# Rotary queries kept by feature: the rotation on whole tiles, heads put together by DMA

## The chip, the cores and the metric

The kernel runs on one core of a Trainium2 chip. The metric is the device time of one execution in microseconds, taken as the median of several runs. The core has a matrix engine (TensorE, PE in the profile; its weight loads are listed as PEld), VectorE (DVE), ScalarE (ACT), GpSimd (POOL) and SyncE (SP), each with an instruction queue of its own that is worked off in order. DMAs are issued from the queues of SP, ACT and POOL.

## The reference, cut to what matters

The reference is one layer with two token mixers side by side, gated linear attention (GLA) and multi-head latent attention (MLA), and a feed-forward block behind them. There are 512 tokens of width 1024. The change concerns MLA's rotary part:

```python
def apply_rope(x, cos, sin):
    half = x.shape[-1] // 2
    xf = x.astype(jnp.float32)
    x1, x2 = xf[..., :half], xf[..., half:]
    return jnp.concatenate([x1 * cos - x2 * sin, x2 * cos + x1 * sin], axis=-1).astype(x.dtype)
...
    q = (rms_norm(q_lat, q_a_norm_g) @ w_q_b).reshape(bsz, seq, MLA_HEADS, MLA_QK)
    q_nope = q[..., :MLA_NOPE]
    q_rope = apply_rope(q[..., MLA_NOPE:], cos[:, :, None], sin[:, :, None])
    c_kv = rms_norm(kv_lat[..., :MLA_KV_RANK], kv_a_norm_g)
    k_rope = apply_rope(kv_lat[..., MLA_KV_RANK:], cos, sin)
...
    s = (jnp.einsum('bhqd,bhkd->bhqk', q_nope[:, :, q0:q1], k_nope[:, :, :q1])
         + jnp.einsum('bhqr,bkr->bhqk', q_rope[:, :, q0:q1], k_rope[:, :q1]))
```

There are eight heads. Each head's query has 128 plain features and 64 rotary ones; `q_lat` has rank 384. The rotary key of 64 features is shared by the heads.

## The kernel before, in words

**Numbers.** Almost every product is made in three matmuls on operands that are split into a high part (rounded by ACT) and a low part (the rest, subtracted by DVE): high by high, high by low, low by high. `split` does this for a tile. Weights come by SP's queue into `wraw`, are split into `whi` (line L189) and `wlo` (L190) by `pump`, which runs ahead of the products by one entry of a list (`stream`), and by two entries with the loads. The buffers for these are two or three each, so a split waits for the product that last read its buffer.

**Two forms of product.** `gemm_fm` keeps the weights as the stationary operand and gives features on the partitions, 512 tokens wide (L245 to L247). `gemm_tm` keeps the activations stationary and gives tokens on the partitions (L279 to L281), for the rotary queries 256 columns wide: four heads of 64. Both collect in PSUM: four banks of the pool `mm` for products and four of the pool `px` for transposes, scores and the like.

**The order of the work.** The program names its steps one by one, with generators (`spawn`, `tick`) that are stepped between the products; a scheduler that estimates durations then fixes the order on each engine, and the engines follow that order. The stages that matter here: the latents with `latents2` (normalisation, rotary key) among the query, key and value projections of GLA, some 80 to 125 us into the run; the GLA levels beside them (`gla_levels`, L849, with POOL's sums L787 and L788); then the gates (`unit`, L1172 to L1174), which end near 307 us; then `mla_qr(0)`, the first group of four heads; `y_gla(0)`, a projection into four PSUM banks; the first pair of heads; `mla_qr(1)`; `y_gla(1)`; three more pairs.

**Rotary queries before.** `mla_qr` makes, for each of four tiles of 128 tokens, the four heads' rotary features side by side (two token tiles share one PSUM bank). `ev_qr` rotates them on DVE with the tables `cs2` and `sn2`, which have tokens on the partitions (L521 to L523), adds on POOL (L524), and splits the result into `q2` (L114, L115), high and low part beside each other for every head. `tr` then turns each head by four PE transposes (L946) with the rounded identity `identr` and copies it on ACT into `QS` (L949): 128 partitions, of which the upper half is the low part. The scores use `QS` as the stationary operand against the two layers of `KK` (L987, L988).

**Rotary key before.** After the rotation the key is rounded twice into `krh` (L634) and its rest put into `krl` beside zeros (L635, cleared by POOL at L632). Each is transposed in four steps (L642, L646) and copied into `KK` (L643, L648): layer 0 holds the high part twice, layer 1 the low part over zeros.

Of the kernel before, what the change touches and what calls it, by code (L numbers as in the profile page):

```python
# [10 lines left out]
F32 = mybir.dt.float32  # L11
F32R = mybir.dt.float32r
# [19 lines left out]
NOPE = 128  # L32
ROPE = 64
HQ = NOPE + ROPE
# [18 lines left out]
def tile_hybrid_block(ctx: ExitStack, tc: tile.TileContext, I, out, dbg=None):  # L53
    nc = tc.nc
# [12 lines left out]
        uid[0] += 1  # L67
        return f"{s}_{uid[0]}"

    TAG_C = ('h0', 'qn', 'PT1', 'res', 'bc', 'T1', 'T2')  # L70
# [58 lines left out]
    ident = ca[:, 0:P]  # L129
# [4 lines left out]
    identr = consts.tile([P, P], F32R, name="identr")  # L134
# [6 lines left out]
    DMA_AHEAD, SPLIT_AHEAD = 2, 1  # L141
    later = {}

    def plan(name, c0, n, k_lo=0, k_hi=None, heads=None, res=False, per=2):
        w = I[name]
        K = w.shape[0] // P
        k_hi = K if k_hi is None else k_hi
        idx = []
        for k0 in range(k_lo, k_hi, per):
            nk = min(per, k_hi - k0)  # L150
            if heads is None:
                src = w.rearrange("(k p) n -> p k n", p=P)
                dmas = [(slice(0, nk), src[:, k0:k0 + nk, c0:c0 + n], None)]
            else:
                hw, h0, nh = heads
                src = w.rearrange("(k p) (h c) -> p k h c", p=P, c=hw)
                cw = n // nh
                dmas = [(kk, src[:, k0 + kk, h0:h0 + nh, c0:c0 + cw], cw) for kk in range(nk)]
            idx.append(len(stream))
            stream.append({"dmas": dmas, "nk": nk, "n": n, "res": res})  # L160
        return {"idx": idx, "nk": k_hi - k_lo, "per": per}

    def fetch(n):
        while st["dma"] < min(len(stream), n):
            e = stream[st["dma"]]
            st["dma"] += 1
            if "src" in e:
                continue
            raw = A([P, e["nk"], T * 2 // e["nk"]], F32, "wraw")
            for sl, src, cw in e["dmas"]:  # L170
                dst = raw[:, sl, :e["n"]]
                if cw is not None:
                    dst = dst.rearrange("p (h c) -> p h c", c=cw)
                nc.sync.dma_start(dst, src)
            e["raw"] = raw

# [33 lines left out]
    def spawn(g):  # L210
        active.append(g)
        return g
# [87 lines left out]
    PL = {}  # L300
# [25 lines left out]
    PL["v", 1] = plan("w_in", C_V + T, T)  # L326

    def plan_qr(g):
        PL["qr", g] = plan("w_q_b", NOPE, 4 * ROPE, heads=(HQ, 4 * g, 4))


    HOME = {"w": ("whi", "wlo"), "r": ("wraw", "wraw"), "a": ("xh", "xl")}
# [187 lines left out]
    def rope(src, cs, sn, dst, tmp, tmp2):  # L520
        vtt(tmp, src, cs, op=ALU.mult)  # L521
        vtt(tmp2[..., 0:32], src[..., 32:64], sn[..., 0:32], op=ALU.mult)
        vtt(tmp2[..., 32:64], src[..., 0:32], sn[..., 32:64], op=ALU.mult)  # L523
        gtt(dst, tmp, tmp2, op=ALU.add)  # L524
# [92 lines left out]
    def latents2():  # L617
        yield from rms_T(LQ, QR, qag, qlT, qld)
        qlT.clear()
        kr = B([P, NT, ROPE], F32, "kr")  # L620
        kt1 = B([P, NT, ROPE], F32, "kt1")
        kt2 = B([P, NT, ROPE], F32, "kt2")
        for tt in range(NT):
            src = lat[tt][:, LKR:LKR + ROPE]
            vtt(kt1[:, tt], src, cs2[:, tt], op=ALU.mult)
            vtt(kt2[:, tt, 0:32], src[:, 32:64], sn2[:, tt, 0:32], op=ALU.mult)
            vtt(kt2[:, tt, 32:64], src[:, 0:32], sn2[:, tt, 32:64], op=ALU.mult)
        vtt(kr, kt1, kt2, op=ALU.add)
# [12 lines left out]
        for tt in range(NT):  # L641
            nc.tensor.transpose(p[:, tt * P:(tt + 1) * P], krh[:, tt].rearrange("p a b -> p (a b)"), identr)  # L642
        act(KK[:, 0, :], f(p), AF.Copy)  # L643
        p = PX(dt=F32R)
        for tt in range(NT):
            nc.tensor.transpose(p[:, tt * P:(tt + 1) * P], krl[:, tt].rearrange("p a b -> p (a b)"), identr)  # L646
        yield
        act(KK[:, 1, :], f(p), AF.Copy)  # L648
        KKs.append(KK)


# [269 lines left out]
    QS = [None] * MH  # L921
    scale = HQ ** -0.5

    def mla_qr(g):
        qst = []

        def ev_qr(a, j, ps):
            src = ps[:, :4 * ROPE].rearrange("p (h c) -> p h c", c=ROPE)
            csb = cs2[:, a, None, :].to_broadcast([P, 4, ROPE])
            snb = sn2[:, a, None, :].to_broadcast([P, 4, ROPE])  # L930
            if a == 0:
                pump(PL["qr", g]["idx"][-1] + 1)
            t1 = B([P, 4, ROPE], F32, "rt1")
            t2 = B([P, 4, ROPE], F32, "rt2")
            with tc.issue_after(st["lo"].ins):
                rope(src, csb, snb, t1, t1, t2)
            q2 = B([P, 4, 2, ROPE], F32R, "q2")
            split(t1, q2[:, :, 0, :], q2[:, :, 1, :], scale=scale)
            qst.append(q2)
        gemm_tm([PL["qr", g]], qlT, 4 * ROPE, ev_qr)  # L940

        def tr():
            for h in range(4):
                p = PX(dt=F32R)
                for tt in range(NT):
                    nc.tensor.transpose(p[:, tt * P:(tt + 1) * P], qst[tt][:, h].rearrange("p a b -> p (a b)"), identr)  # L946
# [700 lines left out]
```

## Time and profile before

| what | value |
|---|---|
| runs | 886.94, 887.67, 888.92 us |
| median | 887.67 us |
| span of the profiled execution | 884.5 us |
| PE busy | 868.1 us, 98% |
| DVE busy | 638.4 us, 72% |
| ACT busy | 473.6 us, 54% |
| POOL busy | 185.7 us, 21% |
| instructions | 13143 |

The profile is that of one execution; its span runs from the first to the last instruction on the core. No separate device time of that execution is given, so the span is set beside the median of the runs, 3.2 us above it. Matmuls overlap in the pipeline, so their durations add up to more than their time; what one costs is read from the distance between the starts of neighbours.

### The profile page before, as it was taken

How to read it: one execution, taken by the hardware profiler on the slowest of the kernel's cores; microseconds unless marked ns; L12 is line 12 of the kernel's file. 1: busy time of each engine (PE TensorE's matmuls, PEld its weight loads, DVE VectorE, ACT ScalarE, POOL GpSimd, SP SyncE). 2: the span in 40 equal slices, each digit the busy share in tenths (PEclk: the TensorE clock that was granted, in tenths of full speed). 3: DMA queues.
4: the chain of work that ended last, by engine and by line, in shares of the span. 5: the costliest groups of instructions: out<-in, count | busy, mean ns of one | idle time of the engine just before them, and what ended most of it. 6: DMA issues, size and time to landing. Idle time of an engine off the chain costs nothing.

```text
span 884.5 us, 13143 instructions
## 1 busy us (share of the span) xinstructions
PE 868.1 (98%) x4916; PEld 760.3 (86%) x4916; DVE 638.4 (72%) x1019; ACT 473.6 (54%) x834; POOL 185.7 (21%) x200
## 2 busy tenths in 40 slices
PE   6999999999999999999999999999999999999996
PEld 5988888889999988888888888988888888889985
DVE  7859879959665646646866797887557646788865
ACT  6556676556475534435654414566357546656820
POOL 1314457854201010100000003004400520141000
PEclk9999999999999999999999999999999999999999
DMA  7995936795737423112307528006941990399312
GB/s 247 283 221 152 324 110 162 229 215 168 215 87 194 144 78 102 54 54 63 99 19 268 191 72 285 1 1 167 291 113 29 261 254 28 85 232 231 121 61 81
DMA packets 91023, 132.50 MB, mean 150 GB/s; under 512 B 8992, under 2 KB 54432, under 8 KB 90960
## 3 DMA queue, kind: packets, MB, share of 16 engines
q1 hardware_dynamic: 70672, 92.36, 32.5%
q0 software_dynamic: 18368, 35.66, 18.8%
q10 hardware_dynamic: 1920, 3.66, 1.2%
q8 instruction: 38, 0.62, 0.3%
q14 instruction: 25, 0.20, 0.1%
HBM read 110.15 MB, written 8.91 MB: 135 GB/s over the span
## 4 chain that ended last, share of the span: by engine, by line
PE 98%; DMA 1%; ACT 0%; DVE 0%; POOLq 0%; issue 0%; DVEq 0%; ACTq 0%
PE mm L247 11%; PE mm L245 11%; PE mm L246 11%; PE mm L279 6%; PE mm L280 6%; PE mm L281 6%; PE mm L1172 4%; PE mm L1174 4%; PE mm L1173 4%; PE px L1460 2%; PE px L1458 2%; PE px L1459 2%; PE px L849 2%; PE mm L1460 2%; PE mm L1458 2%; PE mm L1459 2%
## 5 line engine op out<-in xcount | busy, mean ns | idle before, releaser
L190 DVE TENSOR_TENSOR wlo<-wraw,whi 128x1024 fp32r<-128x1024 f32 (+1 forms) x90 | 100.1, 1112 | 91.4 <-ACT whi L189 86.6
L189 ACT ACTIVATE whi<-wraw 128x1024 fp32r<-128x1024 f32 (+1 forms) x90 | 85.5, 950 | 81.3 <-PE mm L246 34.7
L246 PE MATMUL mm<-h,whi 128*128 128x512 f32 x224 | 87.2, 389 | 0.0
L245 PE MATMUL mm<-h,whi 128*128 128x512 f32 x224 | 87.1, 390 | 0.0
L247 PE MATMUL mm<-h,wlo 128*128 128x512 f32 x224 | 83.2, 390 | 0.0
L190 DVE TENSOR_TENSOR wlo<-wq,whi 128x1024 fp32r<-128x1024 f32 x44 | 54.5, 1239 | 30.0 <-ACT whi L189 30.0
L1477 POOL DMA_DIRECT2D res<-ev x42 | 37.4, 1000 | 180.7 <-ACT ev L1475 151.5
L189 ACT ACTIVATE whi<-wq 128x1024 fp32r<-128x1024 f32 x44 | 46.5, 1057 | 27.1 <-PE mm L1173 19.0
L1173 PE MATMUL mm<-sh,whi 128*128 128x256 f32 x176 | 49.9, 283 | 0.0
L1172 PE MATMUL mm<-sh,whi 128*128 128x256 f32 x176 | 49.9, 283 | 0.0
L1174 PE MATMUL mm<-sh,wlo 128*128 128x256 f32 x176 | 49.8, 283 | 0.0
L247 PEld LDWEIGHTS mm<-h,wlo 128*128 128x128 f32 x224 | 42.0, 188 | 9.1 <-DVE wlo L190 0.4
L246 PEld LDWEIGHTS mm<-h,whi 128*128 128x128 f32 x224 | 42.0, 188 | 8.8
L245 PEld LDWEIGHTS mm<-h,whi 128*128 128x128 f32 x224 | 42.0, 188 | 8.6
L189 ACT ACTIVATE xh<-wraw 128x1024 fp32r<-128x1024 f32 (+1 forms) x28 | 27.5, 987 | 28.0 <-PE mm L281 15.8
L429 POOL TENSOR_TENSOR mv<-mv,mhalf 128x1 f32<-128x1 f32 x4 | 3.3, 837 | 170.4 <-DVE mv L428 170.4
L190 DVE TENSOR_TENSOR xl<-wraw,xh 128x1024 fp32r<-128x1024 f32 (+1 forms) x28 | 31.3, 1129 | 8.7 <-ACT xh L189 8.7
L793 ACT ACTIVATE E<-rp 128x256 f32<-128x256 f32 x64 | 25.8, 418 | 20.5 <-POOL rp L788 13.7
L1520 ACT ACTIVATE relu<-mm 128x512 f32<-128x512 f32 x24 | 14.1, 596 | 42.0 <-PE mm L247 42.0
L788 POOL TENSOR_TENSOR rp<-rp 128x256 f32<-128x256 f32 x32 | 33.0, 1030 | 9.8 <-ACT q L818 6.1
L787 POOL TENSOR_TENSOR rp<-rp 128x256 f32<-128x256 f32 x32 | 29.6, 926 | 25.3 <-ACT E L793 18.1
L1174 PEld LDWEIGHTS mm<-sh,wlo 128*128 128x128 f32 x176 | 33.8, 192 | 0.0
(472 smaller groups left out, 2821.4 us busy)
## 6 DMA issues: line engine op xcount, KB each, us to landing
wraw<-in_w_ff_dram SPq DMA_DIRECT2D x36, 512.0 KB, 4.8
wraw<-in_w_in_dram SPq DMA_DIRECT2D x30, 512.0 KB, 4.7
wq<-in_w_ff_dram POOLq DMA_DIRECT2D x26, 512.0 KB, 9.4
res<-ev POOLq DMA_DIRECT2D x42, 256.0 KB, 9.4
wq<-in_w_in_dram SPq DMA_DIRECT2D x20, 512.0 KB, 6.6
wq<-in_w_in_dram POOLq DMA_DIRECT2D x18, 512.0 KB, 9.9
hsd<-hs SPq DMA_DIRECT2D x16, 256.0 KB, 3.8
xr<-hsd SPq DMA_DIRECT2D x16, 256.0 KB, 3.7
```

What stands on the lines that cost most here:

```text
L189: st["ins"] = act(hi[:, :nk, :n], raw[:, :nk, :n], AF.Copy)
L190: st["lo"] = vtt(lo[:, :nk, :n], raw[:, :nk, :n], f(hi[:, :nk, :n]), op=ALU.subtract)
L245: mm(o, hi[:, c], xh, start=first, stop=False)
L246: mm(o, hi[:, c], xl, start=False, stop=False)
L247: mm(o, lo[:, c], xh, start=False, stop=last)
L279: mm(o, xh, hi[:, :n], start=opens, stop=False, skip_group_check=share)
L280: mm(o, xh, lo[:, :n], start=False, stop=False, skip_group_check=share)
L281: mm(o, xl, hi[:, :n], start=False, stop=last, skip_group_check=share)
L1172: mm(oa, hi[:, k, c], xh, start=opens and k == 0 and a == 0, stop=False, skip_group_check=True)
L1173: mm(oa, hi[:, k, c], xl, start=False, stop=False, skip_group_check=True)
L1174: mm(oa, lo[:, k, c], xh, start=False, stop=k == 3, skip_group_check=True)
L1477: nc.gpsimd.dma_start(res[tt + t][:, j * T:(j + 1) * T], e, accum_op=ALU.add)
```

## The change

The products of the rotary queries are turned round: `gemm_fm` with the weights as the stationary operand, so that features stand on the partitions and 512 tokens in the row. So that the rotation needs no partner from another partition, the weights of a group are loaded in two blocks of 128 columns: the first halves of the four heads' features, then the second halves (`parts=2`, 32 columns of each head to a piece, two DMAs where there was one). Each block's product is one PSUM bank.

The rotation is then made on whole tiles of 128x512 with tables that have features on the partitions. `tables` makes them once, ahead of the first group: ACT repeats cosine and sine for four heads, PE transposes them in eight steps with the plain identity, ACT copies them into one tile `tab` of the tag C, which also holds other large tiles. DVE makes two products and a sum for each half (the sum was POOL's), and `split` gives the high and low parts, four tiles `q2`.

The heads are put together by 16 DMAs a group from POOL's queue, each moving 32 partitions of a `q2` tile, 64 KB, into a `QS` tile. The transposes of the queries and their ACT copies are gone.

The rotary key is transposed once, before it is split: four transposes of 64 features, two ACT copies for the two halves of layer 0, one DVE subtraction for the low part. POOL clears the lower half of layer 1.

```diff
     def fetch(n):
...
             for sl, src, cw in e["dmas"]:
-                dst = raw[:, sl, :e["n"]]
-                if cw is not None:
-                    dst = dst.rearrange("p (h c) -> p h c", c=cw)
+                if cw is None:
+                    dst = raw[:, sl, :e["n"]]
+                else:
+                    dst = raw[:, sl[0], sl[1]].rearrange("p (h c) -> p h c", c=cw)
                 nc.sync.dma_start(dst, src)
...
     def plan_qr(g):
-        PL["qr", g] = plan("w_q_b", NOPE, 4 * ROPE, heads=(HQ, 4 * g, 4))
+        PL["qr", g] = plan("w_q_b", NOPE, 4 * ROPE, heads=(HQ, 4 * g, 4), parts=2)
...
-        krh = B([P, NT, 2, ROPE], F32R, "krh")
-        krl = B([P, NT, 2, ROPE], F32R, "krl")
-        nc.gpsimd.memset(f(krl[:, :, 1, :]), 0.0)
-        for i in range(2):
-            act(krh[:, :, i, :], kr, AF.Copy)
-        vtt(krl[:, :, 0, :], kr, f(krh[:, :, 0, :]), op=ALU.subtract)
-        yield
         yield from rms_T(LKV, KVR, kvg, ckT, ckd)
         ckT.clear()
         KK = A([P, 2, T], F32R, "KK")
-        p = PX(dt=F32R)
+        nc.gpsimd.memset(f(KK[ROPE:, 1, :]), 0.0)
+        p = PX()
         for tt in range(NT):
-            nc.tensor.transpose(p[:, tt * P:(tt + 1) * P], krh[:, tt].rearrange("p a b -> p (a b)"), identr)
-        act(KK[:, 0, :], f(p), AF.Copy)
-        p = PX(dt=F32R)
-        for tt in range(NT):
-            nc.tensor.transpose(p[:, tt * P:(tt + 1) * P], krl[:, tt].rearrange("p a b -> p (a b)"), identr)
-        yield
-        act(KK[:, 1, :], f(p), AF.Copy)
+            nc.tensor.transpose(p[:ROPE, tt * P:(tt + 1) * P], kr[:, tt], ident)
+        yield
+        for i in range(2):
+            act(KK[i * ROPE:(i + 1) * ROPE, 0, :], p[:ROPE], AF.Copy)
+        vtt(KK[:ROPE, 1, :], p[:ROPE], f(KK[:ROPE, 0, :]), op=ALU.subtract)
         KKs.append(KK)
...
+    tabs = []
+
+    def tables():
+        tab = A([P, 2, T], F32, "tab")
+        for i, (src, c0) in enumerate(((cs2, 0), (sn2, 32))):
+            p, w = PX(), B([P, NT, 4, 32], F32, "tabw")
+            act(w, src[:, :, None, c0:c0 + 32].to_broadcast([P, NT, 4, 32]), AF.Copy)
+            for tt in range(NT):
+                nc.tensor.transpose(p[:, tt * P:(tt + 1) * P], w[:, tt].rearrange("p a b -> p (a b)"), ident)
+            act(tab[:, i], p, AF.Copy)
+        tabs.append(tab)
+
     def mla_qr(g):
...
-        gemm_tm([PL["qr", g]], qlT, 4 * ROPE, ev_qr)
-
-        def tr():
+        if g == 0:
+            tables()
+        cos, sin = tabs[0][:, 0], tabs[0][:, 1]
+        ps = []
+
+        def ev_qr(a, p):
+            ps.append(p)
             if a == 0:
                 pump(PL["qr", g]["idx"][-1] + 1)
...
+                return
+            parts = []
+            for i, (x, y, op) in enumerate(((ps[0], ps[1], ALU.subtract), (ps[1], ps[0], ALU.add))):
+                t1 = B([P, T], F32, "rt1")
+                t2 = B([P, T], F32, "rt2")
+                with tc.issue_after(st["lo"].ins):
+                    vtt(t1, x, cos, op=ALU.mult)
+                    vtt(t2, y, sin, op=ALU.mult)
+                    vtt(t1, t1, t2, op=op)
+                q2 = [B([P, T], F32R, "q2") for _ in range(2)]
+                split(t1, *q2, scale=scale)
+                parts.append(q2)
             for h in range(4):
-                p = PX(dt=F32R)
-                for tt in range(NT):
-                    nc.tensor.transpose(p[:, tt * P:(tt + 1) * P], qst[tt][:, h].rearrange("p a b -> p (a b)"), identr)
-                yield
                 q = B([P, T], F32R, "QS")
-                act(q, f(p), AF.Copy)
+                for w in range(2):
+                    for i in range(2):
+                        r = (2 * w + i) * 32
+                        nc.gpsimd.dma_start(f(q[r:r + 32]), f(parts[i][w][32 * h:32 * h + 32]))
                 QS[4 * g + h] = q
-        return spawn(tr())
+        gemm_fm(PL["qr", g], qlT, 4 * ROPE, ev_qr)
```

Counted over the whole program: PE loses 72 matmuls of 256 columns and 40 rounded transposes and gains 36 matmuls of 512 columns and 12 plain f32 transposes; POOL loses 8 sums and gains 32 DMA issues; SP issues 12 DMAs for these weights where it issued 6.

More of the change, by code (lines that the diff above doesn't have):

```diff
@@ L68, in nm @@
         return f"{s}_{uid[0]}"
-    TAG_C = ('h0', 'qn', 'PT1', 'res', 'bc', 'T1', 'T2')
+    TAG_C = ('h0', 'qn', 'PT1', 'res', 'bc', 'T1', 'T2', 'tab')
     TAG_W = {'wraw': 3, 'whi': 2, 'wlo': 2}
@@ L142, in tile_hybrid_block, with plan @@
     later = {}
-    def plan(name, c0, n, k_lo=0, k_hi=None, heads=None, res=False, per=2):
+    def plan(name, c0, n, k_lo=0, k_hi=None, heads=None, res=False, per=2, parts=1):
         w = I[name]
@@ L156, in plan @@
                 src = w.rearrange("(k p) (h c) -> p k h c", p=P, c=hw)
-                cw = n // nh
-                dmas = [(kk, src[:, k0 + kk, h0:h0 + nh, c0:c0 + cw], cw) for kk in range(nk)]
+                cw, np_ = n // nh // parts, n // parts
+                dmas = [((kk, slice(i * np_, (i + 1) * np_)), src[:, k0 + kk, h0:h0 + nh, c0 + i * cw:c0 + (i + 1) * cw], cw)
+                        for kk in range(nk) for i in range(parts)]
             idx.append(len(stream))
@@ L922, in tile_hybrid_block @@
     scale = HQ ** -0.5
-    def mla_qr(g):
[L925 to L930, printed above, removed]
+    tabs = []
[8 more added lines that the diff above has]
+        tabs.append(tab)
@@ L931, in ev_qr @@
+    def mla_qr(g):
+        if g == 0:
[4 more added lines that the diff above has]
+            ps.append(p)
             if a == 0:
                 pump(PL["qr", g]["idx"][-1] + 1)
[L933 to L938, printed above, removed]
@@ L939, in ev_qr @@
-            qst.append(q2)
-        gemm_tm([PL["qr", g]], qlT, 4 * ROPE, ev_qr)
-        def tr():
+                return
[10 more added lines that the diff above has]
+                parts.append(q2)
```

## The prediction, made before the changed kernel ran

> **What bounds the kernel now.** I read the page first: busy time by engine, the slices, the chain that ended last.
>
> ```profile
> PE 868.1 (98%) x4916; PEld 760.3 (86%) x4916; DVE 638.4 (72%) x1019; ACT 473.6 (54%) x834; POOL 185.7 (21%) x200
> PE   6999999999999999999999999999999999999996
> PEclk9999999999999999999999999999999999999999
> PE 98%; DMA 1%; ACT 0%; DVE 0%; POOLq 0%; issue 0%; DVEq 0%; ACTq 0%
> ```
>
> The matrix engine, PE, is 98% of the chain and 9 tenths or more busy in every slice but the first and last; its granted clock is full throughout. Next I asked whether that holds in the stages that the change touches: busy time by windows.
>
> ```profile
> core 0: us, PE busy (x) PEld busy (x) DVE busy (x) ACT busy (x) POOL busy (x), PEclk, DMA share, GB/s
> 80.00:125.00 45.00, 45.00 (x245) 38.50 (x244) 38.02 (x72) 27.18 (x59) 17.59 (x21) 1.00 0.76 253
> 285.00:311.80 26.80, 26.80 (x226) 26.80 (x225) 16.14 (x18) 15.13 (x25) 0.00 (x0) 1.00 0.44 143
> 345.00:386.00 41.00, 41.00 (x242) 35.21 (x241) 24.60 (x60) 18.64 (x42) 3.04 (x4) 1.00 0.19 61
> ```
>
> The rotary key's stage (80 to 125), the end of the gates with the first query group (285 to 311.8) and the second group with what follows it (345 to 386) have PE busy throughout. So an instruction taken from PE shortens the span by its interval, one added lengthens it, and work on VectorE (DVE), ScalarE (ACT) or GpSimd (POOL) counts only if PE must wait for it. Intervals are read from start to start in the timeline, because durations overlap.
>
> **PE's stream, term by term.**
>
> ```profile
> 307.46 0.40 PE L279 MATMUL mm<-whi,latT 128*128 128x256 f32 x2
> 307.70 0.28 PE L280 MATMUL mm<-wlo,latT 128*128 128x256 f32 x1
> 317.35 0.39 PE L247 MATMUL mm<-ogT,wlo 128*128 128x512 f32 x1
> 317.58 0.39 PE L245 MATMUL mm<-ogT,whi 128*128 128x512 f32 x1
> 317.80 0.39 PE L246 MATMUL mm<-ogT,whi 128*128 128x512 f32 x1
> 320.07 0.40 PE L247 MATMUL mm<-ogT,wlo 128*128 128x512 f32 x1
> 320.31 0.79 PE L946 MATMUL px<-identr,q 128*128 128x128 f32 x8
> 320.93 0.46 PE L245 MATMUL mm<-ogT,whi 128*128 128x512 f32 x1
> ```
>
> The products: each group has 36 matmuls 256 wide before (3 blocks of the rank, 4 token tiles, 3 parts) and 18 that are 512 wide after. Two of the narrow take 307.70 - 307.46 = 0.24 us, one 0.12; the wide one takes (317.80 - 317.35)/2 = 0.225. 72 x 0.12 = 8.64 against 36 x 0.225 = 8.10: **-0.5 us**.
>
> The query transposes: eight take 320.93 - 320.31 = 0.62 us, all 32 are removed: **-2.5**.
>
> ```profile
> 104.01 0.60 PE L569 MATMUL px<-ca,lat 128*128 128x128 f32 x4
> 104.37 0.48 PE L280 MATMUL mm<-wlo,h 128*128 128x512 f32 x1
> 109.83 0.52 PE L642 MATMUL px<-identr,krh 128*128 128x128 f32 x4
> 110.18 0.49 PE L646 MATMUL px<-identr,krl 128*128 128x128 f32 x4
> 110.52 0.74 PE L849 MATMUL px<-M 128*128 128x64 f32 x5
> ```
>
> The key: its eight transposes take 110.52 - 109.83 = 0.69; the four plain f32 ones that replace them are bounded by the four at L569, 104.37 - 104.01 = 0.36: **-0.3**. The tables: two times four f32 transposes of that form, 2 x 0.36: **+0.7**. PE's own work is thus 0.5 + 2.5 + 0.3 - 0.7 = 2.6 us shorter.
>
> **What the tables wait for.** They need two ACT copies of cosine and sine, which the build puts behind the second L1188 copy; the first four transposes stand 26 matmuls into the product that begins at 297.0, behind the last matmul of the one before:
>
> ```profile
> 296.90 0.28 PE L1174 MATMUL mm<-sh,wlo 128*128 128x256 f32 x1
> 296.98 0.58 ACT L1188 ACTIVATE u<-mm 128x512 f32<-128x512 f32 x1
> 297.46 0.90 ACT L1212 ACTIVATE gt<-u,hbg 128x256 f32<-128x256 f32 x2
> 298.96 1.06 ACT L189 ACTIVATE whi<-wq 128x1024 fp32r<-128x1024 f32 x1 [0.60 <-PE mm L1173]
> ```
>
> A copy of that size takes 0.58, so both are done near 297.5 + 2 x 0.6 = 298.7; PE arrives at 297.0 + 26 x 0.12 = 300.1. Cost: nothing, hidden by 1.4 us; the gate functions and the L189 split behind them move back inside ACT's 0.60 of idle time and the slack of a product. If that cover were gone the price is at most the two copies, 1.2.
>
> **The new wait I expect.** The query group's two PSUM banks must come free before the next projection (y_gla, L1272) can open its third and fourth. Before, the first bank was freed by six small DVE operations; after, both banks are read by both halves of the rotation, and DVE's order is cosine product, sine product, sum, low part, and the same again. The third bank waits for the second cosine product, the fourth for the last sine product.
>
> ```profile
> 313.07 1.22 DVE L190 TENSOR_TENSOR wlo<-wraw,whi 128x1024 fp32r<-128x1024 f32 x1 [0.22 <-ACT whi L189]
> 314.21 0.42 DVE L521 TENSOR_TENSOR rt<-mm,cs 128x256 f32<-128x256 f32 x1
> 315.47 0.28 DVE L523 TENSOR_TENSOR rt<-mm,sn 128x128 f32<-128x128 f32 x1
> 364.38 0.48 PE L245 MATMUL mm<-ogT,whi 128*128 128x512 f32 x1
> L1190 DVE TENSOR_TENSOR u<-mm,u 128x512 f32<-128x512 f32 x6 | 4.1, 684 | 0.0
> L1059 DVE TENSOR_TENSOR hraw<-h 128x512 f32<-128x512 f32 x8 | 6.3, 825 | 0.0
> ```
>
> The first bank was free at 315.47 + 0.28 = 315.75, and PE opened the third projection bank at 317.58: no wait. Now from 314.21: two products of 128x512 from PSUM, 0.6 to the next start (0.68 long with 0.08 overlap, as L190 and L521 overlap) and 0.68, to 315.5; the sum 0.68 (the L1059 row, one stalled instance apart) to 316.2; ACT's high part 0.6 to 316.8; the low part 0.6 to 317.5; the second cosine product 0.68 to 318.2. PE asks at 317.58, since both chains start from the group's last matmul. **+0.6 us**, between 0 (the chain 0.6 quicker) and 1.2 (if the third bank had to wait for the sine product too). In the second group DVE does the same chain among softmax work, but PE reaches the third bank only after a block of scores, at 364.38, when DVE has had some 9 us since the group's last product (its 36 start at 347.31, the row further down, with scores between them); I cost it at nothing. Queued on PE behind the bank wait are 24 matmuls of y_gla, then everything.
>
> **Other edits.** DVE loses small operations and gains large ones of the same element count; ACT loses eight 128x512 evacuations and gains four such for the tables; POOL loses the eight sums of L524. All lie beside PE. Clearing half of the key tile now stands inside POOL's chain for the first GLA head, where a memset delays a level by up to 0.52:
>
> ```profile
> L779 POOL MEMSET rp<- x4: 516/523/1042, 79.4 to 180.6; 128x512 f32 x4
> ```
>
> That is 0 to 0.5 on PE. PE's order between 80 and 125 is rearranged by the scheduler as well; as that stage had no idle PE at all, it can only lose: 0 to 1. I take 0 for both and keep 1.5 for the range.
>
> **Copies on the POOL queue.** 32 copies of 64 KB put the heads together, 16 for each group, in an order in which the first head needs the 13th. The build reuses eight semaphores in turn, so a copy waits for the one eight before it.
>
> ```profile
> L1477 POOL DMA_DIRECT2D res<-ev x42 | 37.4, 1000 | 180.7 <-ACT ev L1475 151.5 <-DMA res<-ev 22.7 <-DMA wq<-in_w_ff_dram 3.7
> res<-ev POOLq DMA_DIRECT2D x42, 256.0 KB, 9.4
> 345.63 0.27 PE L987 MATMUL px<-KK,QS 128*128 128x128 f32 x1
> ```
>
> The nearest row issues one in 1.0 us and lands 9.4 us later, with four times the bytes and an addition, so 9.4 is a high estimate. From 318 the 13th goes out at 318 + 4 + 9.4 = 331.4 at the latest and lands at 340.8; PE reads QS at 345.63, some 2 us earlier after the savings above. Hidden by 3 us on the dear end. The second group's copies have until head 4, two pairs of heads later. On POOL nothing else is queued until the next layer norm.
>
> The Trainium skill, page "SBUF — State Buffer", section "SBUF: two separate sides", speaks against this place: a copy issued by GpSimd has its descriptors written there, and a VectorE instruction holding the shared port keeps it from writing them. The row above of 1.0 us an issue was taken beside a busy DVE; by the rule the first head's copies would come later still, which is the slow rival below.
>
> **Weight loads.** The group's weights now come in 128-byte pieces, twice as many: six DMAs instead of three for a group. Their landing in the two piece sizes of before:
>
> ```profile
> wraw<-in_w_q_b_dram SPq DMA_DIRECT2D x3, 128.0 KB, 2.4
> wraw<-in_w_q_b_dram SPq DMA_DIRECT2D x1, 128.0 KB, 2.2
> L174 SPq DMA_DIRECT2D wraw<-in_w_q_b_dram x18: 367/368/548, 275.3 to 403.9; - x18
> 336.63 3.19 SPq L174 DMA_DIRECT2D wraw<-in_w_q_b_dram  x3
> 347.31 0.36 PE L279 MATMUL mm<-whi,latT 128*128 128x256 f32 x1
> ```
>
> The first is the window 336.6 to 340 (256-byte pieces), the second 357.2 to 357.6 (512-byte pieces): half the piece, hardly later. If each of the three more took its 2.4 us behind the others, the queue would be 7.2 us longer. The first group is loaded from 275.3 for use at 307.46. The second is issued from 336.63 and used from 347.31: its first block, two DMAs landed by 336.63 + 0.4 + 2.4 = 339.4 before, is there by 339.4 + 2 x 2.4 = 344.2 at the dearest. Hidden by 3 us less a split of about 1.3 in the tighter place. The Trainium skill, "DMA: Bandwidth & Descriptors", section "Specifications", asks for 512 bytes and more and says that smaller writes are read, modified and written; the two rows do not show that price, and I keep the rows.
>
> **Rivals.** (a) *The bank wait does not appear*, because DVE's chain is 0.6 quicker: -2.6, 885.1. For: my chain adds full lengths at four handovers. Chance 0.15. (b) *The saving is eaten by waits in the rearranged PE order* (80 to 125, or the second group): another 1.5, -0.4, 887.3. For: every place had PE full with a fixed order, so any slip shows; against: no other resource there is above 85%. Chance 0.25. (c) *Slower: the copies are late for the first head.* The 13th copy lands at 322 + 2L for a landing time of L; it decides from L = 10.8 us, where that reaches 343.6. At L = 14 it lands at 350, PE waits 6.4, and the sum is -2.0 + 6.4 = +4.4, 892.1. For: deep queue, DVE busy; against: 9.4 for four times the bytes. Chance 0.08. A smaller loss of the kind of (b), 3 us and more of waits, has 0.07.
>
> **How the numbers follow.** Forecast, 0.45: -2.6 + 0.6 = -2.0. The profiled span, 884.5, lies 3.2 under the median 887.67; that difference lies outside the span and stays. The span goes to 882.5, the median to 885.7. I count 0.2%, 1.8 us, as what a measurement here tells from no change. The forecast lies so near it that 0.65 of its chance is faster and the rest the same. Faster 0.45 x 0.65 + 0.15 = 0.44; same 0.45 x 0.35 + 0.25 = 0.41; slower 0.15. The range: from (a) less 0.8 for spread, 884.3, to (b) with its full 1.5 and 1.5 more, 888.8; what is left out is (c) and little else.
>
> **What would show it.** Right: no L946 in the trace, PE's matmuls of the group at 0.225, eight table transposes without a wait, one wait of about 0.6 at y_gla's third bank for DVE's cosine product, the heads' QS read without a wait. Wrong: PE waiting for QS (then c), for the tables, or at the GLA levels between 80 and 125 (then b), or a landing of the copies above 10 us.

## The result and the profile after

The changed kernel takes 885.08 us, the median of five runs (884.47 to 885.59), against 887.67 for the kernel before in the same comparison (886.94 to 889.19, five runs): a ratio of 0.9968, with a 95% interval of 0.9956 to 0.998. It is faster by 0.32%. The profiled execution has a span of 883.3 us and took 885.08 itself, so 1.8 us lie outside the span.

The page of after: busy time by engine, the granted clock by slices, and the chain that ended last by engine.

```profile
PE 865.6 (98%) x4852; PEld 755.5 (86%) x4852; DVE 637.8 (72%) x1003; ACT 469.4 (53%) x824; POOL 196.9 (22%) x224
PEclk9999999999999999999999999999999999999999
PE 97%; DVE 1%; ACT 1%; DMA 1%; POOLq 0%; issue 0%; SPq 0%; DVEq 0%; ACTq 0%
```

PE is still the bound, at full clock, with 64 matmuls fewer and 2.5 us less busy time. The three stages of the prediction, as windows of after:

```profile
core 0: us, PE busy (x) PEld busy (x) DVE busy (x) ACT busy (x) POOL busy (x), PEclk, DMA share, GB/s
80.00:125.00 45.00, 45.00 (x242) 38.09 (x241) 37.40 (x71) 26.26 (x55) 18.59 (x22) 1.00 0.76 251
285.90:313.10 27.20, 27.20 (x214) 26.48 (x213) 16.16 (x17) 16.94 (x30) 0.00 (x0) 1.00 0.45 140
345.60:384.20 38.60, 38.60 (x204) 32.30 (x203) 25.05 (x53) 16.05 (x36) 7.99 (x16) 1.00 0.32 91
```

They are as full as before, so what came off PE's stream came off the time.

A span is a blunt measure here: those of the two profiles, 884.5 and 883.3 us, differ by only 1.2. A span also holds the start, where PE waits 8.3 to 9.4 us for the first input, depending on the profile, and that scatter is larger than several of the effects sought. So I compare the time between the same matmuls in both traces. The first fence has rows of PE's timeline of before (the start of the query group and of the first head are in the prediction), the second those of after: the last `vh` matmul ahead of the gates, the query group's first product, the first product of `y_gla(0)`, the first head's first `QS` matmul, and the last one of all heads.

```profile
251.76 0.28 PE L894 MATMUL px<-vh,sd 128*128 128x256 f32 x1
311.78 0.40 PE L245 MATMUL mm<-ogT,whi 128*128 128x512 f32 x1
454.48 0.39 PE L988 MATMUL px<-KK,QS 128*128 128x512 f32 x1
```

```profile
252.42 0.28 PE L888 MATMUL px<-vh,sd 128*128 128x256 f32 x1
308.98 0.40 PE L247 MATMUL mm<-latT,whi 128*128 128x512 f32 x1
313.09 0.39 PE L247 MATMUL mm<-ogT,whi 128*128 128x512 f32 x1
345.85 0.28 PE L995 MATMUL px<-KK,QS 128*128 128x128 f32 x1
452.88 0.39 PE L996 MATMUL px<-KK,QS 128*128 128x512 f32 x1
```

| from, to | before | after | difference |
|---|---|---|---|
| last `vh` to first query product (the tables) | 55.70 | 56.56 | +0.86 |
| to first product of `y_gla(0)` (first group's products) | 4.32 | 4.11 | -0.21 |
| to first `QS` matmul (transposes out, bank wait in) | 33.85 | 32.76 | -1.09 |
| to last `QS` matmul (second group) | 108.85 | 107.03 | -1.82 |
| whole stretch | 202.72 | 200.46 | **-2.26** |

The whole stretch is called S below. Ahead of it the same comparison gives -0.03 for the stage with the key (first latent transpose to first product of split weights with `xr`), but the first latent transpose itself stands 0.68 later in after. Behind S, after takes 430.41 us to the end of the span where before takes 430.05. The ten kernels with the new queries (after among them) are all longer there than before, by 0.07 to 0.71, so a small part of S's gain, 0.07 at least, is lost again; the rest of that difference scatters.

**The tables.** PE's timeline of after, at the two sets of transposes:

```profile
299.72 0.60 PE L926 MATMUL px<-ca,tabw 128*128 128x128 f32 x4
300.07 0.36 PE L1182 MATMUL mm<-sh,wlo 128*128 128x256 f32 x1
300.27 0.28 PE L1180 MATMUL mm<-sh,whi 128*128 128x256 f32 x1
302.79 0.60 PE L926 MATMUL px<-ca,tabw 128*128 128x128 f32 x4
```

No wait is shown. Four transposes take 300.07 - 299.72 = 0.35, and the product behind them takes 0.20 to the next start instead of 0.12. That second part, 0.08 in the product behind, is not in the prediction. Twice 0.43 is the +0.86.

It is no price on top of the transposes. PE's timeline of before has two such groups of four f32 transposes, and the second of them is the row from which the prediction took its price:

```profile
102.27 0.60 PE L569 MATMUL px<-ca,lat 128*128 128x128 f32 x4
102.71 1.47 PE L832 MATMUL px<-x,qk 128*128 128x192 f32 x8
104.69 0.39 PE L281 MATMUL mm<-whi,h 128*128 128x512 f32 x1
```

Where small matmuls follow, they take 102.71 - 102.27 = 0.44. Where a product follows, they take 0.36, and that product takes 104.69 - 104.37 = 0.32 instead of 0.23, which again makes 0.45 together. A distance that ends at a product's start therefore shows too little of the transposes' cost.

**The bank wait.** DVE and PE of after, from the timelines:

```profile
312.80 2.36 DVE L192 TENSOR_TENSOR wlo<-wraw,whi 128x1024 fp32r<-128x1024 f32 x2 [2.86 <-PE mm L248]
315.08 0.68 DVE L946 TENSOR_TENSOR rt<-mm,tab 128x512 f32<-128x512 f32 x1
316.39 0.69 DVE L948 TENSOR_TENSOR rt<-rt,rt 128x512 f32<-128x512 f32 x1
317.78 0.69 DVE L115 SCALAR_TENSOR_TENSOR q<-rt,q 128x512 fp32r<-128x512 f32 x1 [0.70 <-ACT q L114]
318.39 0.68 DVE L946 TENSOR_TENSOR rt<-mm,tab 128x512 f32<-128x512 f32 x1
```

```profile
318.52 0.39 PE L249 MATMUL mm<-ogT,wlo 128*128 128x512 f32 x1
319.13 0.50 PE L247 MATMUL mm<-ogT,whi 128*128 128x512 f32 x1 [0.22 <-DVE rt L946]
319.46 0.39 PE L248 MATMUL mm<-ogT,whi 128*128 128x512 f32 x1
```

The wait is there, at the third bank and for the second cosine product: the next start comes 0.61 after the last one where 0.23 is usual, so it costs 0.38. The product behind the wait then takes 0.33, another 0.10, so the wait costs 0.48 in all.

**The copies.** One line's view of the issuing line on POOL, and its last row:

```profile
L957 POOL DMA_DIRECT2D QS<-q x32: 496/497/651, 318.0 to 371.4; - x32
DMA to landing us min/median/max: 1.8/1.9/4.9
```

They are issued in 0.5 us and land in 1.9, and PE reads `QS` without a wait.

### The profile page after: what moved, and what is told of

Read it like the earlier page. It is cut to its first block, busy times and chain, and to the rows that moved or that the text cites. A ratio compares the mean times of both kernels' runs of the same rounds, so it can differ in the third digit from the quotient of the medians.

```text
span 883.3 us, 13060 instructions
## 1 busy us (share of the span) xinstructions
PE 865.6 (98%) x4852; PEld 755.5 (86%) x4852; DVE 637.8 (72%) x1003; ACT 469.4 (53%) x824; POOL 196.9 (22%) x224
## 4 chain that ended last, share of the span: by engine, by line
PE 97%; DVE 1%; ACT 1%; DMA 1%; POOLq 0%; issue 0%; SPq 0%; DVEq 0%; ACTq 0%
PE mm L247 11%; PE mm L248 11%; PE mm L249 11%; PE mm L283 5%; PE mm L281 5%; PE mm L282 5%; PE mm L1180 4%; PE mm L1182 4%; PE mm L1181 4%; PE px L1468 2%; PE px L1467 2%; PE px L1466 2%; PE px L843 2%; PE mm L1467 2%; PE mm L1468 2%; PE mm L1466 2%
## 5 line engine op out<-in xcount | busy, mean ns | idle before, releaser
L957 POOL DMA_DIRECT2D QS<-q x32 | 15.9, 505 | 86.4 <-ACT q L114 83.6
```

## The experiments

Each profile was read by S, beside the times. Each kernel ran together with the kernel before on the same chip, and the median of those runs of before stands beside it; S is taken from the profiled execution.

| kernel | median, us | before, run beside it | S, us | S against before |
|---|---|---|---|---|
| after | 885.08 | 887.67 | 200.46 | -2.26 |
| key alone | 887.10 | 887.19 | 202.76 | +0.04 |
| queries alone | 885.37 | 887.19 | 200.45 | -2.27 |
| banks freed early | 884.68 | 887.19 | 200.03 | -2.69 |
| tables twice | 885.90 | 887.19 | 201.40 | -1.32 |
| before, transposes twice | 889.84 | 887.35 | 205.35 | +2.63 |
| copies twice, one queue | 889.82 | 887.35 | 204.79 | +2.07 |
| copies on SP | 884.96 | 887.35 | 200.52 | -2.20 |
| tables from four transposes | 884.70 | 887.35 | 200.19 | -2.53 |
| copies twice, two queues | 884.42 | 887.28 | 200.45 | -2.27 |
| both improvements, new key | 884.54 | 887.28 | 199.63 | -3.09 |
| both improvements, old key | 883.62 | 887.28 | 199.64 | -3.08 |

S repeats within 0.01 us for three kernels with the same PE work in it (after, queries alone, copies on two queues). The medians do not: against the before that ran beside it, queries alone is -1.8 and copies on two queues -2.9. So differences of some tenths are read from S and not from the medians.

### The key by itself

Before, with `krh`, `krl` and their two sets of transposes replaced by

```
p = PX()
for tt in range(NT):
    nc.tensor.transpose(p[:ROPE, tt * P:(tt + 1) * P], kr[:, tt], ident)
...
for i in range(2):
    act(KK[i * ROPE:(i + 1) * ROPE, 0, :], p[:ROPE], AF.Copy)
vtt(KK[:ROPE, 1, :], p[:ROPE], f(KK[:ROPE, 0, :]), op=ALU.subtract)
```

> The kernel before with the key change alone. Theory T (as the trace of after reads, where the key's stage ends level with before): the 0.35 us taken from the matrix engine by four f32 transposes for eight rounded ones is lost again to waits in the changed order of 80 to 125 us, so the time is that of before within 0.1 us and the step to the last vh transpose is 0.0. Rival K (the prediction's step): the key saves 0.3 us, step -0.3, and the loss in after came from its other edits. By T the whole difference of -2.6 belongs to the queries.

Ratio 0.9995 (0.9987 to 1.0004); the step over the key's stage is 0.00. The times alone could not tell 0.3 us from nothing; by the step, rival K is out. The saving is not missing, it is spent. Summed from start to start on PE, from 80 us to the same `xr` product:

| us on PE | before | key alone |
|---|---|---|
| key transposes (8, 4) | 0.69 | 0.43 |
| level matmuls (96) | 9.77 | 9.44 |
| `x`, `qk` matmuls (16) | 2.47 | 2.20 |
| products (208) | 48.58 | 49.41 |
| with the 20 latent transposes, 2.02 in each | 63.52 | 63.50 |

The scheduler has put the small matmuls elsewhere. In the timeline of before, 32 of a level stand in one row; in after, as in this kernel, groups of eight stand singly among the products:

```profile
114.92 3.18 PE L849 MATMUL px<-M 128*128 128x64 f32 x32
118.04 0.50 PE L279 MATMUL mm<-whi,h 128*128 128x512 f32 x1
```

```profile
108.63 1.00 PE L843 MATMUL px<-M 128*128 128x64 f32 x8
109.44 0.48 PE L281 MATMUL mm<-whi,h 128*128 128x512 f32 x1
109.76 0.39 PE L282 MATMUL mm<-wlo,h 128*128 128x512 f32 x1
109.99 0.39 PE L283 MATMUL mm<-whi,h 128*128 128x512 f32 x1
```

The first product behind a group takes 0.32 to the next start (109.76 - 109.44) instead of 0.23 (109.99 - 109.76), about 0.09 more. Between 80 and 125 us PE returns to the products 6 times before and 12 times with the new key, which is some 0.5 of the 0.83 us by which the products grew. The other 0.3 was not traced to a row. Against this the level matmuls and the `x`, `qk` matmuls, as many as before, take 0.33 and 0.27 less: as at the transposes above, a group of small matmuls counts shorter where a product follows. So the new order cost 0.83 - 0.60 = 0.23 in all, and that took back the 0.26 of the key's own transposes. Over the six returns more this is 0.04 each, not 0.09.

### The queries by themselves

After, with the key of before put back.

> The changed kernel with the key made as before: only the queries are by feature. Theory T: -2.3 us from the matrix engine's stream against before (products -0.45, transposes -2.66, tables +0.87, bank wait +0.38, less what the switches of kind cost), so the time of after within 0.2. Rival K: 0.3 us slower than after, since the key's part is missing.

S is that of after to 0.01 us. By S, and by the key's step of 0.00, the whole gain is the queries'. The median, 885.37, is 0.3 above that of after, as rival K has it, but the two were not run side by side and the intervals of their ratios to before overlap (0.998, 0.9971 to 0.9989, here; 0.9956 to 0.998 for after), so the times do not decide.

### The bank wait taken away

```
-            parts = []
+            parts, prods = [], []
...
-                    vtt(t2, y, sin, op=ALU.mult)
+                    last = vtt(t2, y, sin, op=ALU.mult)
+                prods.append((t1, t2, op))
+            for t1, t2, op in prods:
+                with tc.issue_after(last.ins):
                     vtt(t1, t1, t2, op=op)
```

> The changed kernel, with all four products of VectorE made before the sums and low parts, so that both PSUM banks of a query group come free two operations sooner. Theory T: the second bank's last reader moves from about 319.0 to about 317.0 us, the wait of 0.38 us in the first group at the next projection's third bank goes, nothing else moves: 0.4 us faster than after. Rival B: the matrix engine then stands at something else that is late there (the split of the next weights, which shares VectorE), and the time is that of after. Head copies go out some 1 us later than in after, still far ahead of their use.

DVE's timeline of this kernel shows the four products in a row:

```profile
316.19 0.68 DVE L946 TENSOR_TENSOR rt<-mm,tab 128x512 f32<-128x512 f32 x1
316.79 0.68 DVE L947 TENSOR_TENSOR rt<-mm,tab 128x512 f32<-128x512 f32 x1
317.38 1.29 DVE L951 TENSOR_TENSOR rt<-rt,rt 128x512 f32<-128x512 f32 x2
```

The second cosine product ends at 316.87 instead of 319.07, PE's products run on at 0.23, and S is 0.43 shorter than after's. The stretch that holds the bank wait is 0.53 shorter (32.23 instead of 32.76), of which 0.48 was the wait and the product behind it. The second group is 0.09 longer; PE's order changed there too, so this is not assigned. The gain is shown by S alone: the median is -2.5 against before, where after has -2.6. In this profile PE also waits some 0.2 us for split weights at two places outside S, at 148.75 and 797.50, where after does not.

### The tables' price

`tables()` is called in both groups: a repeat.

> The changed kernel with the transposed tables made a second time, ahead of the second query group (a repeat of work). It measures what the tables cost by themselves. Theory T: eight f32 transposes, 0.35 per four and some 0.08 for each change back to the other kind of matmul, 0.87 us more than after if their two copies by ScalarE are again in time. Rival: the tables cost the path only their 0.7 of transposes (then +0.7), or the copies are late among the softmax work of ScalarE there (then +1 to +2, with a wait of the matrix engine for tabw).

S is 0.94 longer than after's, and PE waits for nothing new. The higher figure holds: a set costs 0.43 to 0.47 with what it adds to the product behind it, and the copies hide even beside the softmax.

### The transposes' price

In before:

```
-                for tt in range(NT):
+                for tt in list(range(NT)) * 2:
```

> The kernel before, with each of the 32 query transposes made twice, one behind the other, into the same place (a repeat of work; the key is left alone). It prices the transposes without removing them. Theory T1 (the prediction's term): the price is the instructions' own interval, 0.62 us for eight, so 32 more take 2.5 us, and their removal can't bring more. Theory T2: in after the two places where query transposes went are 1.47 and 1.48 us shorter when the bank wait and the products are taken out, 2.95 together, which is 0.45 more than T1: each run of transposes also has a fixed price of about 0.11 for the two changes of kind at its ends. By T2 the repeat, which adds no change of kind, costs 2.5 all the same, and the rest is in the first matmul behind the transposes. Rival R: the repeat is hidden or lengthens less than 2 us, and the gain of after has another source.

S grows by 2.63, the median by 2.5. Rival R is out. 32 transposes cost 2.63, or 0.082 each, a little over the 0.0775 that the row of eight gave. Taking them out brought more, about 3.1. Summed by kind from start to start in before, the 32 transposes themselves take 1.25 us in the first group and 1.24 in the second, 2.49 together. The rest is in the products of `y_gla` around them. In the first group the two behind transposes take 0.31 and 0.30 instead of 0.23, together 0.15. In the second, where the transposes stand in shorter runs, the `y_gla` products sum to 0.49 less in after, with 7 instead of 13 of them at 0.28 or more. That is T2's account in kind; its price of 0.11 for a run of transposes is not shown by itself.

The profiled execution of this kernel, at 896.89 us, was hit by a late weight load near 543 us, far behind S. It is of use for one thing, in its windows:

```profile
543.60:546.80 3.20, 0.01 (x1) 0.00 (x0) 0.00 (x0) 0.24 (x1) 0.00 (x0) 1.00 1.03 388
546.80:548.50 1.70, 0.00 (x0) 0.00 (x0) 0.86 (x1) 1.70 (x4) 0.00 (x0) 0.51 1.03 373
548.50:553.60 5.10, 5.03 (x15) 4.04 (x16) 4.61 (x11) 3.78 (x9) 0.00 (x0) 0.50 1.01 359
```

In a pause of 5 us the granted clock fell to half after 3.2 us, and behind it PE ran for 5 us more at 0.50. Behind S this profile takes 437.58 us where before takes 430.05, so pause and slow stretch cost 7.5.

### Copies twice on one queue

```
+                        for _ in range(2):
                             nc.gpsimd.dma_start(f(q[r:r + 32]), ...)
```

> The changed kernel with every copy that puts the heads together issued twice (a repeat of work): 64 on the POOL queue instead of 32. Theory T: POOL issues one in 0.5 us and each lands in about 2 us, so the first group's 32 are out by about 318 + 16 = 334 us and landed by 337, 8 us ahead of the first head's scores; time and matrix engine's steps as in after within 0.1 us. Rival C (copies late): the copies stand near the edge, so twice as many push the first head out and the matrix engine waits for QS, 2 us or more.

Theory T failed, yet not in rival C's way: the median is 4.7 us above that of after (5.1 when each is set against its own before), and S is 4.33 longer. POOL's timeline has the last of the first group's copies, PE's the first head:

```profile
337.71 0.50 POOL L958 DMA_DIRECT2D QS<-q  x1 [1.36 <-DMA QS<-q]
```

```profile
350.90 0.22 PE L996 MATMUL px<-KK,QS 128*128 128x128 f32 x1
352.50 0.23 PE L998 MATMUL px<-negb,identb 128*128 128x128 bf16 x1
355.36 0.30 PE L1017 MATMUL px<-ca,P 128*128 128x128 f32 x1 [2.62 <-DVE sme L1004]
357.67 0.63 PE L248 MATMUL mm<-ogT,whi 128*128 128x512 f32 x1
358.09 0.63 PE L249 MATMUL mm<-ogT,wlo 128*128 128x512 f32 x1
```

At the median landing of 2.0 us the copies are there by 340, some 11 us before the first `QS` matmul, and PE does not wait for `QS`. The scheduler has moved these matmuls back in PE's order: after has them from 345.85, between the products of the next projection. Here the products are used up first, four rows of scores come within 1.6 us, and PE has nothing left beside the softmax of DVE and ACT. It stands still for 2.6 us. Then the windows of this kernel; the first ends where the granted clock falls, the second where it is full again:

```profile
353.40:356.80 3.40, 1.44 (x13) 1.43 (x14) 3.32 (x13) 1.57 (x5) 0.00 (x0) 1.00 0.69 223
356.80:360.20 3.40, 3.40 (x11) 2.76 (x11) 2.94 (x10) 1.73 (x7) 0.00 (x0) 0.50 0.01 2
```

At the granted clock of 0.50 the products go out every 0.42 us (358.09 - 357.67) instead of 0.23, for 3.4 us. In the 3.4 us ahead of the fall PE had been busy for 1.44. The pause costs 2.6 us and the slow stretch half of its 3.4, 1.7; together these are the 4.3.

The Trainium skill, "TensorE: Matmul & The Clock Gate", section "HAM oscillation — how this bites in real kernels", has this as a rule: no idle gaps of the matrix engine over some 3.4 us, or the next work starts at half clock. Both profiles agree on the half clock (0.50), and the pause of 5 us agrees on the length, with the fall 3.2 us into it. The pause of this kernel does not: a gap of 2.6 us was enough, and the fall came only 1.4 us after PE had resumed.

### The head copies on SP

> The changed kernel with the head copies issued on SP's queue, where the weights are loaded, instead of POOL's. Theory T: an issue there takes 0.37 us (the weight loads' row), and in the first group the 16 copies wait for VectorE between about 318 and 321 us with the next weights' loads queued behind them for up to 3 us; the weights are ahead by more than that, so the time is that of after within 0.2. Rival Q: the loads queued behind the copies come late, and the matrix engine waits for the split of wraw, 1 us or more; then the choice of the POOL queue is part of the gain.

In the line of the edit `nc.gpsimd.dma_start` becomes `nc.sync.dma_start`. S is 0.06 longer than after's, the median 884.96, and no weight comes late. The choice of POOL's queue is worth nothing here.

### One set of transposes for both tables

```
+        p, w = PX(), B([P, NT, 4, 32], F32, "tabw")
...
+            act(w[:, :, i::2, :], src[...].to_broadcast([P, NT, 2, 32]), AF.Copy)
+        for tt in range(NT):
+            nc.tensor.transpose(p[:, tt * P:(tt + 1) * P], w[:, tt]..., ident)
+        for h in range(4):
+            for i in range(2):
+                r = ((h // 2) * 2 + i) * 32
+                dst, src = tab[32 * h:32 * h + 32, i], p[r:r + 32]
...
```

> The changed kernel with both tables out of one set of four transposes: the tile that is transposed holds cosine, sine, cosine, sine, and eight copies of 32 partitions, by ScalarE and VectorE, spread the result. Theory T: four f32 transposes and one change of kind less on the matrix engine, 0.43 us faster than after, if the eight small copies are done before the first rotation (they have some 10 us). Rival: the eight copies, longer together than the two of before, delay ScalarE's or VectorE's split of the next weights and the matrix engine waits for that, and the gain is gone.

Ahead of the first group the step is +0.43 where after has +0.86: the set saved. S gains only 0.27, for the bank wait has grown. The first cosine product on DVE and PE at the third bank, in this kernel:

```profile
314.60 0.69 DVE L953 TENSOR_TENSOR rt<-mm,tab 128x512 f32<-128x512 f32 x1
317.93 0.39 PE L249 MATMUL mm<-ogT,wlo 128*128 128x512 f32 x1
318.66 0.50 PE L247 MATMUL mm<-ogT,whi 128*128 128x512 f32 x1 [0.34 <-DVE rt L953]
```

A start distance of 0.73 less 0.23 is 0.50 where after loses 0.38. PE did not just come earlier to the same wait, for DVE's chain moved forward with it. But that chain starts 2.15 us behind the first product of `y_gla(0)` (312.45 here), where after has 315.08 - 313.09 = 1.99. It is 0.16 later by itself; which of the eight small copies or other operations ahead of it did this was not traced.

### The same copies on two queues

```
+                        for e in (nc.gpsimd, nc.sync):
+                            e.dma_start(f(q[r:r + 32]), ...)
```

> The changed kernel with every head copy issued twice again, but once on POOL's queue and once on SP's (a repeat of work). The matrix engine's order is the same as in after, instruction by instruction, where the repeat on one queue had moved the first head's scores some 5 us back in that order. Theory O (order): the 4.7 us of the repeat on one queue came from that moved order, in which four softmax rows come at once and the matrix engine has nothing left to do beside them; the same 64 copies in the old order cost nothing: the time of after within 0.2. Theory L (load): the copies themselves, twice the traffic beside VectorE's and ScalarE's work, cost it: again 3 to 5 us more than after, with the matrix engine waiting for QS or for VectorE.

The median is 884.42, S 200.45: theory O. One line's view of this kernel:

```profile
L958 POOL DMA_DIRECT2D QS<-q x32: 498/498/575, 317.9 to 371.3; - x32
L958 SPq DMA_DIRECT2D QS<-q x32: 507/532/1084, 319.9 to 381.7; - x32
```

PE's order is that of after, matmul by matmul, and the same 64 copies cost nothing in it. As PE did not wait for `QS` on one queue either, the 4.7 us were the order's. That the scheduler moved the scores because it reckons with a longer queue is the natural reading; no run here shows what it reckoned.

### Both improvements together

Banks freed early and one set of transposes, with the new key and with the old.

> The changed kernel with both improvements together: the four products ahead of the sums (bank wait gone, -0.43) and the tables out of four transposes (-0.43). Theory T: they add up, -0.86 against after, and -3.1 against the median of before made of its steps. Rival: the tables' eight small copies delay the group's rotation (the single look at four transposes had 0.15 more of bank wait), and the sum is -0.6 or less.

> The same with the key made as before. Theory T: the key's part is worth nothing, so this is within 0.1 us of its twin with the new key. The matrix engine returns to the products 6 times instead of 12 between 80 and 125 us in that case, 0.09 us each, and does eight rounded transposes instead of four: 0.83 + 0.26 on both sides of the account as in the run with the key alone. Rival K: the new key is worth 0.3 when nothing else disturbs it.

S is 0.83 and 0.82 shorter than after's: with the bank wait gone, the set of transposes counts in full (0.43 + 0.43 were expected). The medians are 884.54 (ratio 0.9966, 0.9954 to 0.9979) and 883.62 (0.9961, 0.9947 to 0.9974); after had 0.9968. By S both beat both kernels; by the times alone the step from after is within the intervals. The two differ by 0.9 in the median and by 0.01 in S. The new key's profile takes 0.94 more than before between 144 and 223 us, most of it at one wait of PE for split weights at 188.56, where the other kernels take 0.01 to 0.35 more. So this difference is not put down to the key, and whether the old key is better by anything stays open.

## Why the prediction was right, point by point

- **PE bounds, so PE's stream is the time.** Right. In all eleven further kernels the median moved as S did, within 0.6 us. With the copies on one queue S itself grew, by a pause of PE that a new order brought.
- **Products, -0.5.** Measured -0.21 in the first group and, summed by kind, -0.14 in the second. Right, a little high.
- **Query transposes, -2.5.** About -3.1 were taken out. The instructions were priced rightly (2.49). The term left out the products around them, which take 0.6 less without them.
- **Key, -0.3.** Wrong: 0.0. The instructions got cheaper by 0.26, as reckoned. But the order was rearranged, PE returned to the products twice as often, and the new order cost 0.23. The prediction had this as rival (b), "waits in the rearranged order"; it was no wait for a resource, but the price of the order, and it ate this term only.
- **Tables, +0.7.** Measured +0.86; the missing part is 0.08 for each set, in the product behind it. The row of 0.36 ended at a product's start and so showed too little.
- **The tables' wait, 0.** Right, with less cover than the 1.4 of the prediction. ScalarE's timeline of after:

```profile
298.12 0.62 ACT L924 ACTIVATE tabw<-cs 128x512 f32<-128x512 f32 x1
298.64 0.62 ACT L924 ACTIVATE tabw<-sn 128x512 f32<-128x512 f32 x1
```

  The second is done at 299.26, 0.46 ahead of the first transpose.
- **Bank wait, +0.6.** Right in place and cause; in size 0.38, or 0.48 with the product behind it. DVE's chain took the 4.0 us that the prediction had added up, from 315.08 to the end of the second cosine product at 319.07, so the four handovers were summed rightly. But it began 1.99 us behind the first product of `y_gla(0)`, where the prediction's 314.21 is 2.43 behind it (311.78): the two weight splits ahead of it end earlier in after, where they stand back to back; before, DVE waited 0.22 between them. That both chains start from the group's last matmul was not so. Freed early, the wait goes.
- **Second group's bank wait, memset, 0.** No wait of PE for either is shown.
- **Copies hidden.** Right, with far more room: they land in 1.9 us, at most 4.9, where the estimate was 9.4 and rival (c) began at 10.8. The rule of the Trainium skill on the shared port ("SBUF — State Buffer", section "SBUF: two separate sides"), by which VectorE's work would hold the issues up, is not seen: the longest issue of 32 took 0.651 against a median of 0.497, with DVE busy 65% of the second group's window. Whether any of these DVE instructions holds that port no run here shows.
- **Weight loads.** Right. The 128-byte pieces of the second group, in the window 336 to 342 of after:

```profile
wraw<-in_w_q_b_dram SPq DMA_DIRECT2D x6, 64.0 KB, 2.6
```

  They land in 2.6 us, where the 256-byte pieces took 2.4. In the first group they took 4.8, and the larger pieces 5.9.

The sum was -2.0 and S moved by -2.26. That these lie so near each other is in part luck: the misses, 0.6 on the transposes and 0.1 on the bank wait one way, 0.3 on the key, 0.2 on the tables and 0.1 on the products the other way, nearly cancel; about 0.1 is left that was not traced. The median by itself would even speak for rival (a): 885.08 is that rival's 885.1, by which the bank wait does not appear. The trace has the wait, so the forecast's mechanism holds and not rival (a)'s. The 3.2 us that the prediction kept outside the span set one execution's span beside the median of others; where both are known for a run they lie 1.7 to 2.9 apart. The sum was taken off the median, so nothing hangs on it. The median moved by -2.6 in this comparison, and by -1.8 and -2.9 in the two others with S alike; the rest was not traced. The runs of one kernel alone spread over 1.1 us (after) to 2.8 us (before). Part of that can be the start: the first latent transpose stands between 47.56 and 48.85 us in the twelve other profiles, 47.94 in that of before. Both ends belong to kernels with the new queries. Whether these start later on average could not be settled.

## What to carry to other kernels

Where one engine is full, price an edit by its instructions together with the matmul behind them, and by what it does to the order: here a new order cost 0.23 us, enough to turn a saving of 0.26 into nothing. A saving on the full engine can come with a longer wait for another: the set of transposes saved 0.43 and brought 0.27 by itself, and the two edits together brought 0.83, once the wait was removed as well. Before blaming a transfer for a slow-down, compare the order of the bound engine: the same 64 copies cost 4.7 us or nothing, depending on the order that the scheduler made around them.

## What the runs showed of the hardware

- A pause of PE of 2.6 us was followed, 1.4 us after work resumed, by 3.4 us at a granted clock of 0.50; in the 3.4 us ahead of the fall PE had been busy for 1.44. In a pause of 5 us the clock fell after 3.2, and 5 us of work behind it ran at 0.50. The two cost 4.3 and 7.5 us, 1.6 and 1.5 times their length. The 0.38 of the bank wait had no such sequel: one product behind it takes 0.33, and the granted clock stays full.
- A product behind transposes or small matmuls takes 0.08 to 0.09 us more to the next start. Four f32 transposes take 0.44 where small matmuls follow and 0.36 where a product follows, so there the two cancel.
- A copy of 64 KB from one part of on-chip memory to another is issued in 0.5 us on POOL and lands in 1.9, against 1.0 and 9.9 for the `res` copies of 256 KB with addition on the same queue.
